# Splitting h for a three-pass matmul: every second high part cast by ScalarE instead of VectorE

## The chip, the cores and the metric

The kernel runs on one core of one Trainium2 chip. The metric is device time in microseconds (us) of one execution, lower is better. The program holds some 28,000 instructions on five engines: TensorE (PE; PEld are its weight loads), VectorE (DVE), ScalarE (ACT), GpSimd (POOL) and SyncE (SP), which here issues the DMAs.

## What is computed

One inference step of a hybrid backbone with one layer, for 128 context tokens and 2,048 latent tokens of width 1,024 with shared weights. In the reference's words, shortened to what matters here:

```
mod = silu(cond) @ ada_w + ada_b ; shift, scale, gate = split(mod, 3)
h = rmsnorm(x, norm_g) * (1 + scale) + shift
p = h @ w_in                      # 2,832 columns: q,k,v, gates, beta, a, u, v, x_c, x_d ...
y_a = gated DeltaNet over chunks of 64 tokens, both directions
y_b = spatial gating MLP ; y_c = pooling ; y_d = real 2-D DFT
y = x + gate * (concat(y_a, y_b, y_c, y_d) @ w_out) ; final rmsnorm
```

## The kernel before

**Three-pass products.** TensorE multiplies in a reduced float format here (fp32r). For the accuracy of float32 every operand is held as a high part, which is a cast of the value, and a low part, which is the value less its high part. `mm3` (L246) issues three matmuls for each product: high by high, high by low, low by high. All of them have line L250.

**Stages.** The tokens are cut into 17 tiles of 128 (the 17th is the context) and these into three groups of 6, 6 and 5 tiles. `phase_a(gi)` (L892) runs for groups 0, 1 and 2, one after the other: it makes h of the group, multiplies it by the weights (`proj_tm`, `proj_cm`), and prepares the DeltaNet chunks, with convolutions (L824), exponentials (L669, L676, L684), 64x64 products (`pair_pre`), and a triangular solve that is spread over lanes on DVE (`lanes_solve` L725 and L727, transposes L748, copies on ACT L757). In the trace phase A takes about the first 500 us. Behind it come the other branches, mixed with the scan over the chunks (`scan`, L1015, matmuls L1035), and the output projection (`out_tile`, also L250).

**How h is made.** `x_prep` (L322) loads x and normalizes it. `x_fin` (L341) goes over the 8 feature blocks f of 128 columns: TensorE transposes up to 512 tokens (L349), ACT applies scale and shift and writes `h` (L351, a buffer out of 4), `h_split` (L358) writes the high part to `hT[0]` (L361, DVE) and the low part to `hT[1]` (L362; POOL for odd f, DVE for even f), and for groups 0 and 1 a DMA keeps h (L355). The tiles `hT` are a part of `BIG`, and there is one copy of them: the next group's f can be written only when the matmuls of the group before have read it. `x_fin` is called seven times: twice for group 0 (384 and 392 tokens), twice for group 1 (384 and 392), three times for group 2 (384, 128, 128). That makes 56 casts and 56 differences. Below, "the first, second, third block" of a group are these calls.

**Who sets the order.** The kernel is written stage by stage, and a scheduler gives every engine its own fixed order before the program runs, by priorities (`tc.high_priority`) and by its own idea of durations. An engine then executes its order strictly one after the other: what waits holds up all that stands behind it on that engine. A changed duration or a changed engine at one place can therefore move instructions elsewhere in the order.

Of the kernel before, what the change touches and what calls it, by code (L numbers as in the profile page):

```python
# [13 lines left out]
AF = mybir.ActivationFunctionType  # L14
# [130 lines left out]
def tile_dit_step(ctx: ExitStack, tc: tile.TileContext, io: dict, dbg=None, stop=None):  # L145
    nc = tc.nc
# [194 lines left out]
    def x_fin(prep, fs=range(KC), pss=(pc,)):  # L341
        with hp(OXv[0]):
            tiles, off, spill, xts = prep
            w = sum(rows for _, rows in tiles)
            cond = 1 if tiles[0][0] == NTS else 0
            for f in fs:
                ps = pss[f % len(pss)]()
                for j, (i, rows) in enumerate(tiles):
                    nc.tensor.transpose(ps[:, j * 128:j * 128 + rows], xts[j][:rows, f * 128:(f + 1) * 128], ident[:rows, :rows])  # L349
                h = hp_.tile([128, 512], F32, tag="pr", name="h", bufs=4)  # L350
                nc.scalar.activation(h[:, :w], ps[:, :w], AF.Identity, scale=modab[:, 0, f, cond:cond + 1],  # L351
                                     bias=modab[:, 1, f, cond:cond + 1])
                h_split(h[:, :w], f, off)
                if spill is not None:
                    nc.sync.dma_start(out=h_d[spill, :, f, off:off + 384], in_=h[:, :384])  # L355
            return h

    def h_split(h, f, off):  # L358
        w = h.shape[1]
        hi = hT[0][:, f, off:off + w]  # L360
        nc.vector.tensor_copy(hi, h)  # L361
        (nc.gpsimd if f % 2 else nc.vector).tensor_tensor(hT[1][:, f, off:off + w], h, hi.bitcast(F32), op=ALU.subtract)  # L362

    def out_dbg(name, ap):
# [1066 lines left out]
```

## Time and profile before

| what | value |
|---|---|
| median of 3 runs | 1192.86 us (1191.8 to 1195.96) |
| the profiled execution | 1198.78 us, its span 1197.0 us |
| PE busy | 1046.3 us (87% of the span) |
| PEld busy | 954.6 us (80%) |
| DVE busy | 818.9 us (68%) |
| ACT busy | 386.2 us (32%) |
| POOL busy | 433.2 us (36%) |
| chain that ended last, by engine | PE 41%, DVE 27%, DMA 17%, issue 6%, ACT 4% |

A profile is one execution. Its instructions have a start and a duration in us from the span's start. An idle time of an engine is shown with what released it: `[2.62 <-DVE tm L708]` means that the engine sat idle for 2.62 us until the DVE instruction of line 708 that wrote `tm` was done.

### The profile page before, as it was taken

What the parts mean: (1) busy time and instruction counts of PE and PEld (TensorE: products, weight loads), DVE (VectorE), ACT (ScalarE), POOL (GpSimd) and SP (SyncE); (2) the same over time, 40 slices, a digit from 0 to 9 for tenths busy, and PEclk for the clock granted to TensorE, in tenths of its full rate; (3) what the DMA queues carried; (4) which work ended last, traced back from release to release, by engine and by line L of the source; (5) the groups of instructions that cost most, each with busy time, mean ns of one, the idle gap of its engine ahead of it and who ended that gap; (6) DMA issues with size and microseconds to landing.
All of it is one profiled execution on the core that took longest, in us unless ns stands there. A gap on an engine that the chain in (4) does not pass through costs nothing.

```text
span 1197.0 us, 27975 instructions
## 1 busy us (share of the span) xinstructions
PE 1046.3 (87%) x11351; PEld 954.6 (80%) x11351; DVE 818.9 (68%) x1837; ACT 386.2 (32%) x734; POOL 433.2 (36%) x436
## 2 busy tenths in 40 slices
PE   4689897888768789967988999888999889999997
PEld 1489786888757788955778888878899879999997
DVE  1547878699995799958865533672443398887765
ACT  1345566436675564131131111121111311111211
POOL 1338446633562245511132132232144444332212
PEclk7599897898978899988899999999999889999998
DMA  9799557854453655565268356578555655444331
GB/s 309 238 327 290 156 117 202 250 165 112 107 134 103 154 126 126 179 170 160 71 197 241 100 170 207 176 230 283 143 151 161 204 153 186 132 142 140 108 131 71
DMA packets 251395, 204.16 MB, mean 171 GB/s; under 512 B 109150, under 2 KB 218718, under 8 KB 251010
## 3 DMA queue, kind: packets, MB, share of 16 engines
q1 hardware_dynamic: 251266, 202.37, 57.7%
q8 instruction: 89, 1.46, 0.5%
q14 instruction: 40, 0.33, 0.1%
HBM read 138.86 MB, written 63.46 MB: 169 GB/s over the span
## 4 chain that ended last, share of the span: by engine, by line
PE 41%; DVE 27%; DMA 17%; issue 6%; ACT 4%; SPq 2%; POOL 2%; DVEq 0%; ACTq 0%; POOLq 0%
PE pj L250 32%; DMA wst<-in_wt_dram 4%; PE pa L1035 3%; DMA ada<-in_ada_dram 3%; DVE LL L727 3%; DVE acc L824 3%; DVE ltmp L725 3%; DMA pr<-in_cpr_dram 2%; DVE BIG L243 2%; DVE BIG L361 1%; DVE acc L871 1%; SPq L1024 1%; DVE BIG L240 1%; DVE BIG L362 1%; DVE LL L748 1%
## 5 line engine op out<-in xcount | busy, mean ns | idle before, releaser
L250 PE MATMUL pj<-BIG 128*128 128x256 f32 (+4 forms) x3888 | 630.8, 319 | 25.6 <-ACT raw L805 5.6
L250 PEld LDWEIGHTS pj<-BIG 128*128 128x128 f32 x3888 | 578.1, 201 | 50.7 <-issue 11.0
L250 PE MATMUL pj<-BIG,yh 128*128 128x256 f32 x1088 | 196.7, 286 | 1.6 <-ACT BIG L1340 0.8
L243 POOL TENSOR_TENSOR BIG<-wst,BIG 128x512 fp32r<-128x512 f32 (+1 forms) x66 | 93.3, 1414 | 215.2 <-DVE BIG L240 131.2
L250 PEld LDWEIGHTS pj<-BIG,yh 128*128 128x128 f32 x1088 | 164.7, 191 | 4.6 <-ACT BIG L1340 1.0
L250 PE MATMUL pj<-BIG,yl 128*128 128x256 f32 x544 | 140.8, 284 | 0.0
L250 PEld LDWEIGHTS pj<-BIG,yl 128*128 128x128 f32 x544 | 99.0, 191 | 0.4
L240 DVE CAST BIG<-wst 128x512 fp32r<-128x512 f32 (+2 forms) x72 | 35.0, 487 | 75.7 <-DMA wst<-in_wt_dram 35.4
L1398 POOL TENSOR_TENSOR z<-z,xs 128x1024 f32<-128x1024 f32 x16 | 40.3, 2521 | 75.8 <-DVE z L1390 66.0
L1042 POOL TENSOR_TENSOR gS<-S,sc_s 128x256 f32<-128x256 f32 x32 | 19.7, 616 | 132.1 <-DVE S L1057 109.1
L824 DVE SCALAR_TENSOR_TENSOR acc<-raw,prm,acc 128x768 f32<-128x768 f32 (+2 forms) x72 | 66.3, 942 | 1.6 <-ACT acc L822 1.6
L243 DVE TENSOR_TENSOR BIG<-wst,BIG 128x512 fp32r<-128x512 f32 (+1 forms) x66 | 49.8, 754 | 24.3 <-ACT BIG L242 20.7
L1359 ACT ACTIVATE yh<-yt 128x768 fp32r<-128x768 f32 (+1 forms) x34 | 20.5, 628 | 121.6 <-issue 65.5
L1204 ACT ACTIVATE g<-pj 128x256 f32<-128x256 f32 (+1 forms) x64 | 23.0, 397 | 109.6 <-PE pj L250 109.3
L725 DVE TENSOR_TENSOR ltmp<-LL 128x60 f32<-128x60 f32 (+14 forms) x90 | 55.5, 617 | 1.6
L727 DVE TENSOR_TENSOR LL<-LL,ltmp 128x60 f32<-128x60 f32 (+14 forms) x90 | 55.3, 615 | 1.5
L242 ACT ACTIVATE BIG<-wst 128x512 fp32r<-128x512 f32 (+1 forms) x60 | 37.7, 633 | 38.4 <-DMA wst<-in_wt_dram 17.9
L264 PE MATMUL pb<-ada,c 128*32 128x256 f32 x192 | 22.1, 566 | 31.7 <-DMA ada<-in_ada_dram 21.4
L1057 DVE TENSOR_TENSOR S<-pa,gS 128x256 f32<-128x256 f32 x34 | 14.3, 421 | 50.6 <-PE pc L1035 45.3
L1390 DVE TENSOR_TENSOR z<-pj,gbc 128x256 f32<-128x256 f32 x68 | 26.2, 420 | 29.1 <-PE pj L250 28.8
L362 POOL TENSOR_TENSOR BIG<-h,BIG 128x384 fp32r<-128x384 f32 (+2 forms) x28 | 29.1, 1041 | 44.5 <-DVE BIG L361 38.7
L1360 DVE TENSOR_TENSOR yl<-yt,yh 128x768 fp32r<-128x768 f32 (+1 forms) x34 | 40.4, 1206 | 4.1 <-ACT yh L1359 3.9
(280 smaller groups left out, 1690.2 us busy)
## 6 DMA issues: line engine op xcount, KB each, us to landing
wst<-in_wt_dram SPq DMA_DIRECT2D x96, 256.0 KB, 3.7
R<-rec_d SPq DMA_DIRECT2D x136, 128.0 KB, 3.0
ada<-in_ada_dram SPq DMA_DIRECT2D x24, 512.0 KB, 8.7
C<-com_d SPq DMA_DIRECT2D x68, 128.0 KB, 3.2
xs<-xs_d SPq DMA_DIRECT2D x16, 512.0 KB, 5.3
out_dram<-z SPq DMA_DIRECT2D x16, 512.0 KB, 3.0
x<-in_xs_dram SPq DMA_DIRECT2D x13, 512.0 KB, 6.4
xs_d<-x SPq DMA_DIRECT2D x13, 512.0 KB, 4.7
```

Of the source, the lines that this page charges most:

```text
L240: nc.vector.tensor_copy(hi[:, ks, a:a + w], st[:, :, :w])
L242: nc.scalar.activation(hi[:, ks, a:a + w], st[:, :, :w], AF.Copy)
L243: (nc.vector if k0 == 0 else nc.gpsimd).tensor_tensor(lo[:, ks, a:a + w], st[:, :, :w], hi[:, ks, a:a + w].bitcast(F32), op=ALU.subtract)
L250: nc.tensor.matmul(out, lh[a](k), rh[b](k), start=(k == first and i == 0), stop=(k == last and i == 2))
L362: (nc.gpsimd if f % 2 else nc.vector).tensor_tensor(hT[1][:, f, off:off + w], h, hi.bitcast(F32), op=ALU.subtract)
L725: nc.vector.tensor_tensor(tv, X[:, :, j, j + 1:32].unsqueeze(2).to_broadcast([128, 2, j, ni]), bc(X[:, :, 0:j, j], ni), op=ALU.mult)
L727: nc.vector.tensor_tensor(X[:, :, 0:j, j + 1:32], X[:, :, 0:j, j + 1:32], tv, op=ALU.add)
L824: nc.vector.scalar_tensor_tensor(o, raw[:, si + j:si + j + n], w[:, j:j + 1], o, op0=ALU.mult, op1=ALU.add)
L1035: nc.tensor.matmul(ps[o, q], lh(q)[hp], rh[hp, q])
L1360: nc.vector.tensor_tensor(yl[:, q], yt[:, q], yh[:, q].bitcast(F32), op=ALU.subtract)
L1390: nc.vector.tensor_tensor(z[:, ns], ps, gbc[:, cd, ns], op=ALU.mult)
L1398: nc.gpsimd.tensor_tensor(z, z, xs, op=ALU.add)
```

## The change

For even f the high part is written by an ACT instruction (a copy with conversion, from SBUF to SBUF), for odd f by DVE as before. The differences stay where they were: DVE for even f, POOL for odd f.

```
     def h_split(h, f, off):
         w = h.shape[1]
         hi = hT[0][:, f, off:off + w]
-        nc.vector.tensor_copy(hi, h)
+        if f % 2:
+            nc.vector.tensor_copy(hi, h)
+        else:
+            nc.scalar.activation(hi, h, AF.Copy)
         (nc.gpsimd if f % 2 else nc.vector).tensor_tensor(hT[1][:, f, off:off + w], h, hi.bitcast(F32), op=ALU.subtract)
```

So 28 of the 56 casts go from DVE to ACT: 12 of 128x384, 8 of 128x392 and 8 of 128x128. Lines behind L361 move down by 3: L364 is the cast on ACT, L362 that on DVE, L365 the difference. The scheduler also gives another order to instructions that the diff doesn't touch, at many places of the program. Three of them follow.

ACT in group 1, the end of the second block. L351 writes h, L684 (L687 after) is an exponential, L711 (L714) copies values that PE has transposed, L911 (L914) takes a product out of PSUM, L242 casts weights. The two L351 rows ahead of the last L711 are those of f = 6 and 7. Before:

```order
L684 ACTIVATE Pf<-Pf 128x1536
L351 ACTIVATE h<-pc,modab 128x392
L242 ACTIVATE BIG<-wst 128x4x128 x2
L351 ACTIVATE h<-pa,modab 128x392
L711 ACTIVATE tm<-pb 128x2x256
L351 ACTIVATE h<-pc,modab 128x392
L351 ACTIVATE h<-pa,modab 128x392
L711 ACTIVATE tm<-pb 128x2x128
L911 ACTIVATE xdt<-pj 128x256 x3
```

and now:

```order
L687 ACTIVATE Pf<-Pf 128x1536
L351 ACTIVATE h<-pc,modab 128x392
L364 ACTIVATE BIG<-h 128x392
L242 ACTIVATE BIG<-wst 128x4x128
L351 ACTIVATE h<-pa,modab 128x392
L914 ACTIVATE xdt<-pj 128x256
L714 ACTIVATE tm<-pb 128x2x256
L914 ACTIVATE xdt<-pj 128x256 x2
L714 ACTIVATE tm<-pb 128x2x128
```

The h of f = 6 and 7, and the cast of f = 6, stand ahead of both L714 copies now. The h of f = 4 and 5 stand further up, ahead of the exponential.

DVE in group 2, the first block, around the transposes that end the triangular solve of group 1 (L748, L751 after; `XT` and `LL` are its tiles). L605 to L623 (L608 to L626) are small steps on the keys' norms, L824 (L827) a convolution. Before, the difference of f = 4 stood ahead of the transposes:

```order
L362 TENSOR_TENSOR BIG<-h,BIG 128x384
L609 TENSOR_TENSOR kt<-eB_1762,kt 128x12
L610 TENSOR_TENSOR kt<-be_1759,kt 128x24
L623 SCALAR_TENSOR_TENSOR S_1768<-eB_1762,kt 128x12
L748 STREAM_TRANSPOSE XT<-LL 128x32x32 x2
```

and now, where the two L365 rows are the differences of f = 2 and f = 4:

```order
L751 STREAM_TRANSPOSE XT<-LL 128x32x32 x2
L362 CAST BIG<-h 128x384
L827 SCALAR_TENSOR_TENSOR acc<-raw,prm,acc 128x768
L243 TENSOR_TENSOR BIG<-wst,BIG 128x4x136
L751 STREAM_TRANSPOSE LL<-LL 128x32x32
L365 TENSOR_TENSOR BIG<-h,BIG 128x384
L751 STREAM_TRANSPOSE LL<-LL 128x32x32
L362 CAST BIG<-h 128x384
L608 SCALAR_TENSOR_TENSOR kt<-kt,P_1758 128x24
L620 SCALAR_TENSOR_TENSOR Pp_1763<-kt,P_1758 128x24
L827 SCALAR_TENSOR_TENSOR acc<-raw,prm,acc 128x768
L365 TENSOR_TENSOR BIG<-h,BIG 128x384
```

The transposes have moved ahead of two of the differences that PE needs.

ACT at the same place. L757 (L760 after) copies the transposed solution, four pieces at a time. Before:

```order
L602 ACTIVATE kt<-kt,eps 128x12
L603 ACT_TABLE_LOAD
L603 ACTIVATE kt<-kt 128x12
L242 ACTIVATE BIG<-wst 128x4x136
L242 ACTIVATE BIG<-wst 128x4x128
L351 ACTIVATE h<-pc,modab 128x384
L351 ACTIVATE h<-pa,modab 128x384
L757 ACTIVATE XF<-XT 32x2x12x32 x4
```

and now:

```order
L605 ACTIVATE kt<-kt,eps 128x12
L760 ACTIVATE XF<-XT 32x2x12x32 x4
L364 ACTIVATE BIG<-h 128x384
L606 ACT_TABLE_LOAD
L606 ACTIVATE kt<-kt 128x12
L351 ACTIVATE h<-pc,modab 128x384
L242 ACTIVATE BIG<-wst 128x4x136
L351 ACTIVATE h<-pa,modab 128x384
L760 ACTIVATE XF<-LL 32x2x12x32 x4
L364 ACTIVATE BIG<-h 128x384
```

The casts of f = 4 and f = 6 each stand directly behind a set of four copies, which in turn wait for DVE's transposes.

## Rows read from the trace of the kernel before

**Rows 1.** Busy time by stretch: start:end, length, then PE, PEld, DVE, ACT, POOL, PEclk, DMA share, GB/s

```profile
46.00:68.00 22.00, 19.68 (x136) 17.98 (x129) 19.44 (x36) 12.56 (x22) 11.59 (x9) 0.81 0.65 220
68.00:90.00 22.00, 18.48 (x121) 16.79 (x120) 7.91 (x21) 9.93 (x20) 8.99 (x11) 0.92 1.02 351
...
160.00:213.00 53.00, 42.77 (x354) 37.90 (x353) 45.10 (x83) 34.65 (x59) 29.60 (x30) 0.85 0.66 169
213.00:295.00 82.00, 72.75 (x585) 69.15 (x585) 70.02 (x132) 37.00 (x65) 34.72 (x33) 0.94 0.61 172
295.00:375.00 80.00, 60.66 (x406) 54.63 (x405) 71.00 (x140) 49.54 (x83) 41.01 (x46) 0.82 0.50 118
```

**Rows 2.** The same stretches, DVE's casts of line L361 alone

```profile
46.00:68.00 22.00, 4.34 (x8) 0.81 0.65 220
68.00:90.00 22.00, 3.00 (x8) 0.92 1.02 351
...
160.00:213.00 53.00, 10.20 (x16) 0.85 0.66 169
...
295.00:375.00 80.00, 9.46 (x24) 0.82 0.50 118
```

**Rows 3.** Timeline of DVE and POOL: start, duration, engine, line, operation, tiles, shapes

```profile
49.31 1.44 DVE L361 CAST BIG<-h 128x384 fp32r<-128x384 f32 x1
...
365.62 0.22 DVE L361 CAST BIG<-h 128x128 fp32r<-128x128 f32 x1
...
48.93 1.61 POOL L298 TENSOR_TENSOR x<-x,cpc 128x512 f32<-128x512 f32 x1 [0.94 <-DMA x<-in_xs_dram]
```

**Rows 4.** Timeline of ACT: instructions of two widths

```profile
160.07 0.53 ACT L676 ACTIVATE Po<-Po 128x384 f32<-128x384 f32 x1
...
225.75 0.24 ACT L534 ACTIVATE bl<-lg 128x48 f32<-128x48 f32 x1 [0.43 <-DVE lg L912]
```

**Rows 5.** Timeline of ACT, group 1, end of the second block

```profile
202.46 1.49 ACT L684 ACTIVATE Pf<-Pf 128x1536 f32<-128x1536 f32 x1 [3.32 <-DVE Pf L683]
...
208.73 0.60 ACT L711 ACTIVATE tm<-pb 128x512 f32<-128x512 f32 x1 [2.62 <-DVE tm L708]
209.23 0.67 ACT L351 ACTIVATE h<-pc,modab 128x392 f32<-128x392 f32 x1
```

**Rows 6.** Timeline of DVE and PE at the same place

```profile
207.42 0.68 DVE L243 TENSOR_TENSOR BIG<-wst,BIG 128x512 fp32r<-128x512 f32 x1
208.02 0.68 DVE L708 TENSOR_TENSOR tm<-pb,be 128x512 f32<-128x512 f32 x1
...
209.36 0.41 DVE L708 TENSOR_TENSOR tm<-pb,be 128x256 f32<-128x256 f32 x1
209.93 0.42 DVE L361 CAST BIG<-h 128x392 fp32r<-128x392 f32 x1 [0.16 <-ACT h L351]
210.38 1.26 DVE L362 TENSOR_TENSOR BIG<-h,BIG 128x392 fp32r<-128x392 f32 x1
...
212.47 0.32 DVE L912 COPY lg<-pj 128x16 f32<-128x16 f32 x3
...
212.69 11.69 PE L250 MATMUL pj<-BIG 128*128 128x272 f32 x72 [3.30 <-DVE lg L912]
```

**Rows 7.** Timeline of DVE, PE and ACT, group 2, first block

```profile
324.14 0.61 DVE L361 CAST BIG<-h 128x384 fp32r<-128x384 f32 x2
...
335.18 3.81 DVE L748 STREAM_TRANSPOSE XT<-LL 128x1024 f32<-128x1024 f32 x2
...
348.86 1.82 DVE L362 TENSOR_TENSOR BIG<-h,BIG 128x384 fp32r<-128x384 f32 x1
...
350.73 3.09 PE L250 MATMUL pj<-BIG 128*128 128x272 f32 x12 [4.50 <-DVE BIG L362]
...
337.26 3.40 ACT L757 ACTIVATE XF<-XT 32x768 f32<-32x768 f32 x4 [3.19 <-DVE XT L748]
```

**Rows 8.** The chain of waits: start, duration, piece

```profile
1066.33 11.50 PE pj L250 x96
```

## The prediction

> **What bounds the kernel now.** I read the busy time by stretch first, with the same view of line L361 alone beside it, then the timelines of ACT, DVE and PE at the four places where h is made, and the chain of waits last. The program touches h between 46 and 375 us alone, in four stretches. In 46 to 68 DVE is busy 19.44 of 22 us; in 68 to 90 the DMA engines are full (share 1.02) while DVE does 7.91; in 160 to 213, group 1, DVE is busy 45.10 of 53 us and PE 42.77; in 295 to 375, group 2, DVE 71.00 of 80 and PE 60.66 [rows 1]. In the last two PE waits for h while DVE works almost without a gap, and the granted clock is 0.85 and 0.82 there, against 0.94 in the stretch between them. That stretch, 213 to 295, has PE busy for 72.75 of 82 us: there PE comes first, so a start that is earlier by some us is handed on. ACT has 18 us of idle time in the one DVE-bound stretch and 30 in the other [rows 1].
>
> **What is removed.** Casts of L361 occupy DVE for 4.34, 3.00, 10.20 and 9.46 us in the four stretches, 27.0 together [rows 2]. Half of them by count go, so about 13.5 us by their mean. But a cast that nothing disturbs takes 0.30 us for 128x384 (0.61 for two) and 0.22 for 128x128 [rows 3, 7]; 20 x 0.30 + 8 x 0.22 = 7.8 us. The other 5.7 us are casts that wait inside their own duration: the one at 49.31 takes 1.44 us and ends at 50.75, right behind POOL's addition, which runs from 48.93 to 50.54 [rows 3]. Whether these come back depends on what DVE has next.
> The Trainium skill ("SBUF — State Buffer", section "SBUF: two separate sides") says that DVE and GpSimd share one pair of ports as an exclusive lock, for a DVE instruction that uses both ports or has two SBUF inputs. The rows agree with it in the 1.44 us. By that rule the difference that follows, with its two SBUF inputs, would meet the same POOL instruction, the wait would only change its owner, and group 2 below would give 3.0 us where I take 3.5.
>
> **What is added.** 28 instructions on ACT. Nearest rows: 0.53 us for 128x384 from SBUF to SBUF and 0.24 for 48 columns [rows 4]; the line through the two gives 0.31 for 128. So 20 x 0.53 + 8 x 0.31 = 13.1 us on ACT: 4.2 in group 0, 4.2 in group 1, 2.1 + 2.5 in group 2. A copy needs no new table: in the order's rows the casts L242 and L364 stand behind an exponential without an ACT_TABLE_LOAD.
>
> **Group 0 (46 to 90 us): 0.** Up to 58 us DVE is the late one, and it loses half of 4.34 us. But what comes next is a stretch in which the DMA engines are full, with the loads of the next x among what they move [rows 1]. These loads are issued in the order of SP's queue, whose stores of h and x change places here with about the same bytes ahead of them. I take 0, with bounds of (4.34 + 3.00) / 2 = 3.7 us gained, all that DVE loses, and 4.2 us lost, all that ACT gets.
>
> **Group 1 (160 to 213): 3.3 us gained.** PE's 72 matmuls at 212.69 wait for the small copies L912, which stand on DVE behind the casts and differences of the second block [rows 6]. These are late because ACT's h of f = 6, at 209.23, stands behind a copy L711 that waits 2.62 us for DVE [rows 5]. In the new order f = 6 and its cast follow the exponential, which ends at 202.46 + 1.49 = 203.95. Then h 0.67 and the cast 0.53 end at 205.15; on DVE the difference (up to 1.26), L708 (0.68), L243 (0.68), L708 (0.41) and the cast of f = 7 (0.42) end at 208.6, and the L912 with 0.32 at 208.9 [rows 5, 6]. With four hand-overs of 0.1 us, about the 0.16 of DVE's idle time at 209.93 [rows 6], that is 209.3; before it was 212.47 + 0.32 = 212.8. The difference, 3.5 us, I cut to 3.3, since PE may itself be late with the product that L914 takes out of PSUM. The seven other casts put 3.7 us on ACT ahead of this, and take 10.20 / 2 = 5.1 us from DVE. ACT was waiting for DVE as often as the reverse, so I count these two at nothing; the bounds are their full sizes, 3.7 lost and 5.1 gained.
>
> **Group 2 (295 to 375): 3.5 us gained.** PE's last long wait in the first block, 4.50 us, ends with the difference of f = 6, which ends at 350.68 [rows 7]. From the cast of f = 1 at 324.14 to there DVE runs through. In the new order the same work lies between these two, without the casts of f = 2, 4 and 6 and with one weight difference moved behind: 3 x 0.30 + 0.68 = 1.6 us less [rows 6, 7]. The casts of the two small blocks give 8 x 0.22 = 1.8 us, of which the second block's 0.9 lie on DVE's path. By the mean of rows 2 the twelve casts would give 9.46 / 2 = 4.7; by the short ones 4 x 0.30 + 1.8 = 3.0. I take 3.5, nearer to the short ones. What is late next: the difference of f = 2, which before stood ahead of all transposes, now stands behind three of them, 3 x 3.81 / 2 = 5.7 us. With the weight difference (0.68) and some four wide instructions of about 1 us (0.68 for 512 columns) it comes, by this estimate, 11 us behind the cast of f = 1, and 12 to 14 us ahead of f = 6 [rows 6, 7]. In these PE has the matmuls of f = 2 to 5: 3 tiles x 4 features x 3 = 36 at 3.09 / 12 = 0.26 us make 9.3 us [rows 7], so it fits. Bounds: 4.7 gained, and on the other side the second rival.
>
> **Sum.** 3.3 + 3.5 = 6.8 us. Behind 375 us nothing is removed or added; the order differs, and PE's work is the same. On the profiled execution, 1198.78 us, that gives 1192.0. It lies 5.9 us above the median of the runs shown; on that, 1192.86 - 6.8 = **1186.0 us**, 0.6% less. A measurement here tells about 0.3%, 3.6 us, from no change.
>
> **Rivals.**
> 1. *All of DVE's time comes back.* Both DVE-bound stretches hand on the mean price, 5.1 + 4.7, and group 0 its 3.7: 13.5 us, 1179.4. For it: DVE has no gap in group 2. Against it: waits on POOL change owner, and DMA is full in group 0.
> 2. *ACT's queue becomes the late one.* In group 2 the casts of f = 4 and 6 stand behind sets of copies of 3.40 us each, which wait for DVE's transposes (3.19 us at 337.26) [rows 7]. Price: 2 x 3.40, and in group 1 the 3.7 us on ACT: 10.5 lost, less the 3.3 of the moved h: +7.2, 1200.1 us. It decides from the point at which DVE reaches a difference before ACT has its cast. Against it: by the same count of rows some 12 us of DVE's work lie between the third transpose and the difference of f = 6, and some 9 between the first two and that of f = 4, where ACT needs 3.40 + 0.53 for copies and cast. For it: every early h and every new table ahead of these copies uses up that slack.
> 3. *The tail takes it.* In PE's new order 72 more projection matmuls stand ahead of the first scan step; at 11.50 / 96 = 0.12 us [rows 8] it starts 8.6 us later beside the projections. If the scan's own chain set the end, the result would be 1186.0 + 8.6 = 1194.6, no change. Against it: counted in the new order, 984 matmuls of line L250 still stand behind the scan's last step, 118 us of work, so that PE sets the end.
> 4. *Hidden.* DMA and the solve on DVE take the place of every wait removed: 1192.9.
>
> **Chances.** My forecast, a gain between 3.6 and 10 us: 0.40. Rival 1, or something near it: 0.15. Rivals 3 and 4, within 3.6 us: 0.24. Slower by more: 0.21, rival 2 with 0.13 and other shifts of the order, each priced from no row, with 0.08. So faster 0.55, same 0.24, slower 0.21. The range goes from 1175, a little under rival 1 for the 4.2 us or so by which group 0 may add, to 1200, rival 2; I leave out about 2 in 10 on both sides together.
>
> **What would show it.** Right: DVE's busy time falls by 9 to 14 us and ACT's rises by about 13; PE's 72 matmuls of group 1 start 3 us earlier and those behind f = 6 of group 2 about 7 us earlier than before, and this lead is still there at 500 us. The wait of 2.62 us for L708 no longer stands ahead of an h. Wrong: an ACT cast with a long wait in front of it whose difference is what DVE or PE waits for (rival 2); a lead at 375 us that is gone at 640 or 930 (rival 3); or no lead at 213 (rival 4).

## The result: 0.74% slower, and the profile after

| | median | runs | ratio to before, 95% interval |
|---|---|---|---|
| before | 1195.09 us | 20 | |
| after | 1203.79 us (1198.51 to 1210.42) | 20 | 1.0074 (1.0056 to 1.0091) |

The change costs about 8.7 us. I had forecast 1186.0 us with a range of 1175 to 1200: the sign is wrong, and the result lies outside the range. (My base was the median of the first 3 runs; 20 runs put it 2.2 us higher.) The profiled execution after took 1202.52 us, its span 1200.7 us, only 3.7 us more than the one before; single executions of one kernel spread over some 10 us, so sizes below come from many runs or from means over several profiles, and a single profile is used for places.

The page after, busy time of each engine:

```profile
PE 1044.3 (87%) x11351; PEld 955.5 (80%) x11351; DVE 822.7 (69%) x1809; ACT 396.7 (33%) x762; POOL 443.7 (37%) x436
```

ACT has 28 instructions more and is busy 10.5 us longer. DVE has 28 instructions fewer and is busy 3.8 us longer all the same; POOL, with the same instructions, 10.5 us longer. The view by stretch of after, which answers to [rows 1] (columns as there):

```profile
46.00:68.00 22.00, 19.97 (x132) 19.58 (x132) 17.90 (x35) 14.03 (x29) 11.08 (x9) 1.00 0.63 211
160.00:213.00 53.00, 42.96 (x388) 38.15 (x387) 40.66 (x75) 38.12 (x66) 25.58 (x26) 0.87 0.67 166
213.00:295.00 82.00, 74.77 (x578) 72.24 (x579) 73.75 (x135) 38.86 (x70) 38.62 (x37) 0.94 0.65 176
295.00:375.00 80.00, 58.51 (x371) 51.97 (x372) 66.21 (x124) 50.74 (x90) 45.73 (x45) 0.79 0.50 115
```

Where h is made, DVE did get lighter (45.10 to 40.66 us in group 1, 71.00 to 66.21 in group 2). PE got nothing of it: in 295 to 375 it does 58.51 us where it did 60.66. The stretch between, 213 to 295, has DVE at 73.75 after 70.02, which fits work of group 1 that is done later.

The casts on ACT (line L364 of after alone: stretch, length, ACT's busy time):

```profile
46.00:68.00 22.00, 2.06 (x4) 1.00 0.63 211
68.00:90.00 22.00, 2.13 (x4) 0.92 0.96 318
160.00:213.00 53.00, 4.20 (x8) 0.87 0.67 166
295.00:375.00 80.00, 4.25 (x11) 0.79 0.50 115
```

That is 12.6 us for 27 of them (the last lies behind 375 us), against 13.1 forecast for 28.

**Group 1**, timelines of ACT, DVE and PE after, which answer to [rows 5, 6]:

```profile
207.32 1.49 ACT L687 ACTIVATE Pf<-Pf 128x1536 f32<-128x1536 f32 x1 [1.48 <-DVE Pf L686]
208.72 0.66 ACT L351 ACTIVATE h<-pc,modab 128x392 f32<-128x392 f32 x1
209.41 0.53 ACT L364 ACTIVATE BIG<-h 128x392 fp32r<-128x392 f32 x1
...
209.97 1.04 DVE L365 TENSOR_TENSOR BIG<-h,BIG 128x392 fp32r<-128x392 f32 x1 [1.45 <-ACT BIG L364]
...
212.75 0.32 DVE L915 COPY lg<-pj 128x16 f32<-128x16 f32 x3
...
212.96 9.31 PE L250 MATMUL pj<-BIG 128*128 128x272 f32 x72 [1.33 <-DVE lg L915]
```

h of f = 6 does stand right behind the exponential now, but the exponential begins at 207.32 and not at 202.46. So the 72 matmuls start at 212.96 (before: 212.69).

**Group 2**, timelines of ACT, DVE, POOL and PE after, which answer to [rows 7]:

```profile
339.32 0.52 ACT L364 ACTIVATE BIG<-h 128x384 fp32r<-128x384 f32 x1
...
325.90 3.67 DVE L751 STREAM_TRANSPOSE XT<-LL 128x1024 f32<-128x1024 f32 x2
...
330.62 0.71 DVE L243 TENSOR_TENSOR BIG<-wst,BIG 128x544 fp32r<-128x544 f32 x1
...
345.56 0.55 DVE L365 TENSOR_TENSOR BIG<-h,BIG 128x384 fp32r<-128x384 f32 x1
...
360.44 0.92 DVE L319 SCALAR_TENSOR_TENSOR rr<-rt,rr 128x1 f32<-128x1 f32 x1
...
363.91 0.75 DVE L338 TENSOR_SCALAR x<-x,rr 128x1024 f32<-128x1024 f32 x1
...
342.97 5.79 POOL L365 TENSOR_TENSOR BIG<-h,BIG 128x384 fp32r<-128x384 f32 x1
...
331.38 6.65 PE L250 MATMUL pj<-BIG 128*128 128x272 f32 x31 [3.74 <-DVE BIG L243]
...
348.82 1.16 PE L250 MATMUL pj<-BIG 128*128 128x272 f32 x7 [1.76 <-POOL BIG L365]
...
364.71 0.47 PE L349 MATMUL pc<-cm,x 128*128 128x128 f32 x1 [3.88 <-DVE x L338]
```

DVE's difference of f = 6 ends at 346.1, 4.6 us earlier than in [rows 7]. But PE's matmuls wait 3.74 us for a weight difference that now stands behind two transposes, then 1.76 us for POOL's difference of an odd f, which takes 5.79 us, then 3.88 us for the scaled x (L338). What was won on DVE is gone there; the same instruction of the kernel before:

```profile
363.37 0.75 DVE L338 TENSOR_SCALAR x<-x,rr 128x1024 f32<-128x1024 f32 x1
```

**The end.** The chain of waits after, which answers to [rows 8]:

```profile
1072.38 8.69 PE pj L250 x72
...
1082.15 11.53 PE pj L250 x96
```

From there PE runs almost without a gap, as before. So the loss lies ahead of it.

### The profile page after: what moved, and what is told of

Its sections match the earlier page's. It is cut to its first block, busy times and chain, and to the rows that moved or that the text cites. A ratio compares the mean times of both kernels' runs of the same rounds, so it can differ in the third digit from the quotient of the medians.

```text
span 1200.7 us, 27973 instructions
## 1 busy us (share of the span) xinstructions
PE 1044.3 (87%) x11351; PEld 955.5 (80%) x11351; DVE 822.7 (69%) x1809; ACT 396.7 (33%) x762; POOL 443.7 (37%) x436
## 4 chain that ended last, share of the span: by engine, by line
PE 40%; DVE 28%; DMA 17%; issue 6%; POOL 4%; ACT 3%; SPq 2%; DVEq 0%; ACTq 0%; POOLq 0%
PE pj L250 31%; PE pa L1038 3%; DVE ltmp L728 3%; DVE acc L827 3%; DMA pr<-in_cpr_dram 3%; DVE LL L730 3%; DMA wst<-in_wt_dram 3%; DMA ada<-in_ada_dram 2%; DVE BIG L243 2%; DMA yt<-y_d 1%; POOL BIG L243 1%; DVE BIG L240 1%; DVE acc L874 1%; DVE yl L1363 1%; DMA raw_d<-yd 1%
## 5 line engine op out<-in xcount | busy, mean ns | idle before, releaser
L250 PE MATMUL pj<-BIG 128*128 128x256 f32 (+4 forms) x3888 | 627.7, 318 | 27.7 <-DVE BIG L243 6.3
L250 PEld LDWEIGHTS pj<-BIG 128*128 128x128 f32 x3888 | 575.9, 200 | 49.3 <-issue 8.2
L250 PE MATMUL pj<-BIG,yh 128*128 128x256 f32 x1088 | 195.9, 286 | 2.4 <-ACT BIG L1343 1.4
L243 POOL TENSOR_TENSOR BIG<-wst,BIG 128x512 fp32r<-128x512 f32 (+1 forms) x66 | 100.1, 1516 | 216.7 <-DVE BIG L240 121.4
L250 PEld LDWEIGHTS pj<-BIG,yh 128*128 128x128 f32 x1088 | 163.2, 190 | 5.9 <-ACT BIG L1343 1.6
L250 PE MATMUL pj<-BIG,yl 128*128 128x256 f32 x544 | 138.5, 283 | 0.0
L250 PEld LDWEIGHTS pj<-BIG,yl 128*128 128x128 f32 x544 | 97.4, 190 | 0.3
L240 DVE CAST BIG<-wst 128x512 fp32r<-128x512 f32 (+2 forms) x72 | 41.0, 571 | 70.6 <-DMA wst<-in_wt_dram 32.6
L827 DVE SCALAR_TENSOR_TENSOR acc<-raw,prm,acc 128x768 f32<-128x768 f32 (+1 forms) x72 | 64.1, 913 | 0.1
L365 POOL TENSOR_TENSOR BIG<-h,BIG 128x384 fp32r<-128x384 f32 (+2 forms) x28 | 36.8, 1314 | 59.9 <-DVE BIG L362 54.1
L1363 DVE TENSOR_TENSOR yl<-yt,yh 128x768 fp32r<-128x768 f32 (+1 forms) x34 | 49.5, 1475 | 13.5 <-ACT yh L1362 13.5
L242 ACT ACTIVATE BIG<-wst 128x512 fp32r<-128x512 f32 (+1 forms) x60 | 37.8, 634 | 32.3 <-DMA wst<-in_wt_dram 20.4
```

Of the source, the lines that this page charges most:

```text
L240: nc.vector.tensor_copy(hi[:, ks, a:a + w], st[:, :, :w])
L242: nc.scalar.activation(hi[:, ks, a:a + w], st[:, :, :w], AF.Copy)
L243: (nc.vector if k0 == 0 else nc.gpsimd).tensor_tensor(lo[:, ks, a:a + w], st[:, :, :w], hi[:, ks, a:a + w].bitcast(F32), op=ALU.subtract)
L250: nc.tensor.matmul(out, lh[a](k), rh[b](k), start=(k == first and i == 0), stop=(k == last and i == 2))
L827: nc.vector.scalar_tensor_tensor(o, raw[:, si + j:si + j + n], w[:, j:j + 1], o, op0=ALU.mult, op1=ALU.add)
L1363: nc.vector.tensor_tensor(yl[:, q], yt[:, q], yh[:, q].bitcast(F32), op=ALU.subtract)
```

## The experiments

The one line changes two things: where the casts run, and the order of all five engines. To take them apart, a table with the number of each instruction was added to the kernel, and between neighbours on an engine an edge that fixes the order and adds no wait:

```
     with _tile.TileContext(nc, schedule_with_timeline_sim=True) as tc:
         tile_dit_step(tc, io)
+        _pin(tc)
...
+    for n in np.cumsum(todo).tolist():
...
+            tc.add_manual_dep(i, p, mybir.DependencyInfo(mybir.DependencyClass.NoSync, mybir.DependencyReason.DATA), reason="pin")
+        prev[i.engine] = i.name
```

The kernels differ in `h_split` and in this table. "Old" is the order of the kernel before, "new" that of after; a cut is made at one instruction of the whole list. Ratios are to the kernel before on the same chip; its medians there were 1192.7 to 1196.3 us. No run has the table with an unchanged order. That it costs nothing by itself is read from casts_only, which has it and isn't slower, and from weights_first below, which has the new order but for one instruction and lies at 1.0083, where the change without the table lies at 1.0074 and 1.0098.

| kernel | casts on ACT | 0 to 89 us | 89 to 213 | 213 to 375 | 375 to scan | scan to end | median us | ratio (95%) |
|---|---|---|---|---|---|---|---|---|
| casts_only | even f | old | old | old | old | old | 1193.23 | 0.9988 (0.9965 to 1.0010) |
| order_only | none | new | new | new | new | new | 1213.24 | 1.0149 (1.0124 to 1.0174) |
| after_again | even f | new | new | new | new | new | 1204.18 | 1.0098 (1.0063 to 1.0132) |
| head_new | even f | new | new | new | old | old | 1196.69 | 1.0023 (1.0001 to 1.0046) |
| tail_new | even f | old | old | old | new | new | 1195.00 | 1.0000 (0.9976 to 1.0023) |
| new_to_scan | even f | new | new | new | new | old | 1197.07 | 1.0046 (1.0018 to 1.0075) |
| scan_new | even f | old | old | old | old | new | 1199.09 | 1.0052 (1.0031 to 1.0072) |
| group01_new | even f | new | new | old | old | old | 1198.81 | 1.0057 (1.0033 to 1.0082) |
| group0_new | even f | new | old | old | old | old | 1193.21 | 1.0009 (0.9991 to 1.0026) |
| group1_new | even f | old | new | old | old | old | 1197.18 | 1.0044 (1.0020 to 1.0068) |
| group1_late | even f | old | new from 146 | old | old | old | 1198.80 | 1.0024 (1.0000 to 1.0049) |
| group2_new | even f | old | old | new | old | old | 1196.31 | 1.0025 (1.0003 to 1.0048) |
| casts_all | all | old | old | old | old | old | 1192.46 | 0.9979 (0.9956 to 1.0001) |

### Casts and order apart: casts_only, order_only, head_new, tail_new, after_again

> The 28 casts of even f go to ScalarE, and every engine keeps the order of the kernel before for all other instructions (a table with the number of each instruction adds one order-only edge per neighbour on an engine); a cast stands on ScalarE at the place in the whole list that it had on VectorE. Theory 1 (the reshuffled order costs the time, above all behind the last h at 375 us): none of the 8.7 us is there; within 0.3% of the kernel before, or up to 7 us faster. Theory 2 (the casts themselves cost it, in ScalarE's queue): about 8.7 us slower, ratio 1.007. Theory 3 (the order of the first 375 us costs it): as theory 1.

> All 56 casts stay on VectorE, and every engine is held to the order of the changed kernel; a cast stands on VectorE at the place in the whole list that it had on ScalarE. Theory 1 (the reshuffled order costs the time, above all behind 375 us): slower by 8 to 13 us, ratio 1.007 to 1.011. Theory 2 (the casts themselves): within 0.3% of the kernel before. Theory 3 (the order of the first 375 us): as theory 1.

> The change in the first 375 us alone: casts on ScalarE and the changed kernel's order for what the kernel before issues up to its last difference of h; behind that the order of the kernel before. Theory 1 (the loss lies in the order behind 375 us): within 0.3% of the kernel before or faster by up to 7 us. Theories 2 and 3 (casts, or the order of the first 375 us): slower by about 8.7 us, ratio 1.007.

> Casts on ScalarE, the order of the kernel before up to the last difference of h, and behind that the order of the changed kernel. Theory 1 (the loss lies in the order behind 375 us): slower by about 8.7 us, ratio 1.007. Theory 2 (the casts themselves): slower by 8.7 us here and in the two other kernels with casts on ScalarE. Theory 3 (the order of the first 375 us): within 0.3% of the kernel before.

> The changed kernel once more, with the edit written on one line, on the chip of the next three. If the parts add up (a new order of the first 375 us costs about 4 us against the casts alone, the new order behind it about 1.5), it lies 4 us over the kernel before, ratio 1.003 to 1.005; if new head and new tail cost more together than apart, 7 to 10 us over it, ratio 1.006 to 1.009.

Without the reshuffle the casts cost nothing: 0.9988. The order without the casts costs 1.5%, more than the change itself, so theory 2 (the casts, ACT's queue) falls. (order_only's 1.0149 lies above the 1.007 to 1.011 that theory 1 gave.) Where the order costs it, these five don't say: neither half alone reaches the loss, head_new fits neither forecast, and after_again shows that the loss is real, with 1.0098 above both of its forecasts. The page of casts_only:

```profile
PE 1042.8 (87%) x11351; PEld 946.8 (79%) x11351; DVE 805.1 (68%) x1809; ACT 396.8 (33%) x762; POOL 440.4 (37%) x436
```

DVE is 13.8 us less busy than before, just what the mean price of the casts had promised. In the new order the very same 1809 instructions take 822.7 us (821.8 in after_again): 17.6 us more, all of it in longer durations.

### The scan stage: new_to_scan, scan_new, small_eight, scan_early

small_eight has no table; it lets the scheduler order a smaller edit, shown here. scan_early has all casts on ACT and a table whose order behind about 600 us prefers the scan.

```
-        nc.vector.tensor_copy(hi, h)
+        (nc.scalar.activation(hi, h, AF.Copy) if f % 2 == 0 and w == 128 else nc.vector.tensor_copy(hi, h))
```

> Casts on ScalarE; the changed kernel's order for all that the kernel before issues up to its first scan step, the order of the kernel before from there on (the 72 projection matmuls that the change draws ahead of the first scan step are behind it again). Theory 4 (the rest of the loss comes from the scan stage: 72 matmuls fewer lie between the scan steps, and PE waits inside the steps): as the new head alone, ratio 1.000 to 1.004. Theory 5 (it comes from where the new head meets the new order of 375 to 640 us): 7 to 9 us slower, ratio 1.006 to 1.009.

> Casts on ScalarE; the order of the kernel before up to the first scan step (with the 72 projection matmuls that the change draws ahead of it), the changed kernel's order from there on. Theory 4 (the scan stage): slower than the casts alone by 4 to 6 us, ratio 1.002 to 1.005, and PE's idle time from 740 to 880 us is 5 us longer than with the casts alone. Theory 5: no slower than the casts alone, ratio 0.996 to 1.001.

> Only the eight 128x128 casts of even f in group 2 go to ScalarE, and the scheduler orders the program by itself. It again puts 72 projection matmuls ahead of the first scan step, as the change does, while the order of the first 300 us stays nearly that of the kernel before. Theory 4 (the 72 matmuls and the thinner scan stage cost time): slower by 2 to 6 us, ratio 1.002 to 1.005. Rival (only the head's order costs time): ratio 0.998 to 1.001.

> All 56 casts on ScalarE; the order is the kernel before's up to about 600 us, and behind that one in which the scan is preferred, so that 24 projection matmuls fewer stand ahead of its first step. Theory 4 (72 more cost 5 us, so 24 fewer give about 1.5 us): ratio 0.994 to 0.998. Rival (the kernel before already has the scan early enough): as casts_all, 0.997 to 1.000.

small_eight: 1200.41 us, ratio 1.0043 (1.0020 to 1.0066). scan_early: 1194.46 us, 1.0016 (0.9993 to 1.0039), above both of its forecasts.

With eight casts of 0.2 us moved at 345 to 375 us, the program is 0.43% slower; the scheduler again draws 72 projection matmuls ahead of the first scan step. Taken back, as in new_to_scan, the loss halves (1.0046, between the forecasts of theories 4 and 5). Put in alone, as in scan_new, it appears. tail_new is the one that doesn't fit, at 1.0000. The three kernels with the old head and the new scan stage average 1.0032, those with the new head and the old scan stage (head_new, new_to_scan, three_back below) 1.0032 too. From 0.9988 that is 0.44% for either half, and 0.9988 + 0.0044 + 0.0044 = 1.0076, where after shows 1.0074 and after_again 1.0098. With intervals of 0.2% and more to either side, that the halves add up is a reading which the runs allow, not one that they prove.

In time: over the seven profiles of kernels with the 72 matmuls ahead, the scan starts 263.3 us after the last L912 of phase A, over the eleven with the casts moved and the old place 256.6. From the scan's start to the end PE then has 72 matmuls less to do, 8.6 us by [rows 8], but that stretch takes 548.0 us after 549.6. So 6.7 us are paid and 1.6 come back. Where the rest stays shows when the stretch is cut at the scan's last step. The view by stretch of after, then of casts_only (columns as in [rows 1]):

```profile
642.40:1068.90 426.50, 395.80 (x5229) 362.84 (x5228) 243.22 (x634) 74.91 (x167) 140.49 (x123) 0.96 0.58 177
1068.90:1200.70 131.80, 123.54 (x1144) 121.48 (x1134) 90.16 (x262) 24.47 (x47) 32.71 (x24) 0.99 0.32 113
```

```profile
636.20:1051.70 415.50, 388.87 (x5212) 356.81 (x5214) 235.36 (x632) 75.80 (x174) 135.79 (x123) 0.97 0.60 182
1051.70:1192.70 141.00, 132.66 (x1235) 130.62 (x1226) 96.19 (x278) 26.34 (x50) 35.73 (x25) 0.98 0.33 115
```

The 72 matmuls come from behind the scan's last step, and there PE is busy 9.1 us less, near the price (123.6 us after 132.7, in the means). Between the steps stand as many projection matmuls as ever (2,180 after 2,178), yet the scan takes 424.4 us after 416.9, and the two sets of profiles don't overlap: 421.3 to 426.5 against 414.8 to 418.8. Little of these 7.5 us is PE standing idle, 29.9 us after 28.3. PE is busy longer, 394.5 us after 388.6, and so is DVE, 241.6 after 235.5; the granted clock (1 is its full level) is 0.977 after 0.991 in the first 100 us of the scan and 0.951 after 0.966 in the 140 behind them, in the means. (The one profile of the kernel before has 421.5 us from first to last step, so a single execution doesn't show it.) Why nearly the same work between the scan's steps takes longer is open.

scan_new was to show PE's idle time from 740 to 880 us 5 us longer than casts_only; it is 3.2 us longer. In the other direction scan_early found nothing: 24 matmuls fewer ahead of the scan are no gain, 0.4% over casts_all.

### The head: which group's order costs

> Casts on ScalarE; the changed kernel's order for all that the kernel before issues up to the L912 copy that ends group 1's projection (212.8 us), the order of the kernel before from there on. If the head's 4 us come from group 2's order (295 to 375 us): as the casts alone, ratio 0.996 to 1.001. If they come from groups 0 and 1: ratio 1.001 to 1.004. My prediction had group 1's order gain 3.3 us: then ratio 0.994 to 0.998.

> Casts on ScalarE; the changed kernel's order up to the sixth L912 copy (89 us, group 0's h), the order of the kernel before from there on. If the head's 5 us come from the order in which group 0's h, its loads and stores stand: ratio 1.002 to 1.006. If they come from behind it (the kt chain and what follows in 90 to 213 us): as the casts alone, 0.996 to 1.001.

> Casts on ScalarE; the changed kernel's order only between the sixth and the ninth L912 copy (89 to 213 us, with group 1's h), the order of the kernel before ahead of it and behind it. If the late kt chain of 141 to 188 us carries the head's loss: ratio 1.002 to 1.006. If group 0 does: 0.996 to 1.001. By my prediction's step for group 1 alone: a gain of 3.3 us, 0.995 to 0.997.

> Casts on ScalarE; the changed kernel's order only between the first L613 (146 us) and the ninth L912 copy (213 us), where group 1's h is made; the order of the kernel before ahead of it and behind it. If the order around group 1's h carries the loss of group1_new: ratio 1.002 to 1.006. If the stretch from 89 to 146 us does (loads, kt chain of the first pair): 0.997 to 1.001.

> Casts on ScalarE; the changed kernel's order only between the ninth L912 copy (213 us) and the last difference of h (375 us), the order of the kernel before ahead of it and behind it. By my prediction's step for group 2 alone: a gain of 3.5 us, ratio 0.995 to 0.998. If GpSimd's long difference at 343 us and the scaling of x behind it take the gain, as in the changed kernel's trace: 0.998 to 1.003.

Group 0's order costs nothing that can be measured. Group 1's does: group1_new and group01_new lie 0.56% and 0.69% over casts_only, so the step for which I had forecast a gain of 3.3 us is one that loses. In the profile of group1_new the 72 matmuls of [rows 6] are no later than with the casts alone (the last of those L912 ends at 211.7 us in both); the time goes in the stretch behind, from there to the last L912 of phase A, 168.0 us after 165.2. The other profiles agree: about 168 to 172 us in all ten with the new order of group 1, 163 to 167 in those with the old order of both groups (group2_new, with group 2's alone, 168). What fits is DVE's work that is put off: L613 of the first pair stands at 153.5 us in after, behind wide instructions, and at 144.9 in casts_only. But group1_late, which has only half of the stretch, lies in the middle, and three_back, below, moved that very instruction without a gain that can be told. So the stretch is shown, the instruction is not. Group 2's order costs rather than gains, by an interval that just excludes no change to the kernel before.

Two kernels put single places of the new order back. weights_first moves one DVE instruction; three_back also moves the chain around L613 and takes the old order from the scan on.

```
 L601 TENSOR_REDUCE kt<-tm 128x12
+L243 TENSOR_TENSOR BIG<-wst,BIG 128x4x136
 L748 STREAM_TRANSPOSE XT<-LL 128x32x32 x2
 L361 CAST BIG<-h 128x384
 L824 SCALAR_TENSOR_TENSOR acc<-raw,prm,acc 128x768
-L243 TENSOR_TENSOR BIG<-wst,BIG 128x4x136
```

> The changed kernel's order with one instruction moved: on VectorE the weight difference L243 (128x544) that stands behind two 1024-wide transposes L748 in group 2 is put ahead of them, where the kernel before has it. Theory 6 (this place costs group 2 its time: PE's 31 matmuls at 331.4 us wait 3.7 us for it, and the kt chain and GpSimd's work behind them come late with it): those matmuls start 3 to 4 us earlier, the scaling of x L338 at 363.9 is 3 to 6 us earlier too, and the kernel is 3 to 5 us faster than the changed one, ratio to the kernel before 1.003 to 1.007. Rival: GpSimd's difference of 5.8 us at 343 holds PE anyway; the lead is gone by 380 us, ratio 1.007 to 1.010.

> The changed kernel's order with three places put back: the move of weights_first; on VectorE the small kt chain and L613 of group 0's first pair ahead of L682 again; and from the first scan step on the order of the kernel before. Theory 7 (the loss sits in a few places that can be named): as fast as the casts alone, ratio 0.996 to 1.002. Theory 8 (it is spread over many small displacements): 1.003 or more.

weights_first: 1205.72 us, 1.0083 (1.0058 to 1.0108), no better than the changed kernel: the rival is right. three_back: 1199.39 us, 1.0026 (1.0001 to 1.0051), no clear gain on new_to_scan (1.0046) and between the forecasts of theories 7 and 8, nearer to 8. The timelines of PE and POOL of weights_first at the moved instruction show why:

```profile
328.33 4.23 PE L250 MATMUL pj<-BIG 128*128 128x272 f32 x21
334.93 2.64 PE L250 MATMUL pj<-BIG 128*128 128x272 f32 x10 [2.36 <-DVE BIG L362]
...
344.85 4.49 PE L250 MATMUL pj<-BIG 128*128 128x272 f32 x21 [5.54 <-POOL BIG L243]
...
337.25 6.26 POOL L362 TENSOR_TENSOR BIG<-h,BIG 128x384 fp32r<-128x384 f32 x1 [3.88 <-DVE BIG L361]
343.47 1.32 POOL L243 TENSOR_TENSOR BIG<-wst,BIG 128x544 fp32r<-128x544 f32 x1
```

PE's matmuls start 3 us earlier than in after (328.33, not 331.38) and then wait 5.54 us for POOL's weight difference, which stands behind a difference of 6.26 us. The wait changed its place and its owner.

### All casts on ACT: casts_all, casts_all_again

```
-        nc.vector.tensor_copy(hi, h)
+        nc.scalar.activation(hi, h, AF.Copy)
```

> All 56 casts on ScalarE, every other instruction in the order of the kernel before. If VectorE's time is worth something where PE waits for h: VectorE's busy time falls by 10 to 14 us more, and the time by 1 to 4 us against the casts of even f alone, ratio 0.994 to 0.998. If ScalarE's queue becomes the late one: 2 to 6 us more, ratio 1.000 to 1.005. If h is hidden behind other waits: no difference to the casts alone.

> casts_all once more: all 56 casts on ScalarE, the order of the kernel before. If it is faster than the kernel before: ratio 0.996 to 0.999. If the first measurement was chance: 0.999 to 1.002.

casts_all_again: 1191.59 us, 0.9971 (0.9940 to 1.0002). With casts_all's 0.9979 that is a gain of 0.25%, 3 us, and both intervals just touch no change. Against casts_only (0.9988) no gain can be told. casts_all is the fastest kernel of the study, about 1% faster than the change. The page of casts_all has DVE 11.1 us under casts_only:

```profile
PE 1043.2 (88%) x11351; PEld 951.1 (80%) x11351; DVE 794.0 (67%) x1781; ACT 406.6 (34%) x790; POOL 437.7 (37%) x436
```

So taking 25 us of DVE's busy time where PE waits for h is worth some 3 us, if it is worth anything. That other waits stand close behind is the reading that fits; no run tests it.

## Why the prediction was wrong

**What was removed and added: right in the order of before, wrong in the new one.** I had 13.5 us off DVE by the mean of [rows 2] and 13.1 us onto ACT. casts_only shows 13.8 off, so the 5.7 us of waits inside the casts were saved there too, though POOL's busy time rose by 7.2 us. The change itself put 12.6 us on ACT for 27 casts, but DVE's busy time rose by 3.8 us where I had named a fall of 9 to 14 as the sign of being right: the reshuffle gave back more than the casts had taken. The Trainium skill ("SBUF — State Buffer", section "SBUF: two separate sides") says that the port pair that DVE and GpSimd share is held for a whole instruction. By it I had the waits only change their owner; POOL's 7.2 us are in line with that and DVE's 13.8 are not. Both that reading and my step took the order as fixed.

**Group 0, nothing: right.** The first L912 copies came 3.6 us earlier in after, and 0.4 us at 88 us, behind the stretch that DMA fills (share 0.96). group0_new and casts_only can't be told apart.

**Group 1, 3.3 us gained: failed**, at the step that takes "the exponential, which ends at 202.46 + 1.49" from the old trace. The exponential begins 4.86 us later, at 213 us nothing is gained (212.96 after 212.69), and behind it group 1's order costs 0.56%. The exponential waits for DVE's products, and these for the kt chain (the small steps on the keys' norms), which was moved by the same reshuffle. The reduction at its head, before and then after:

```profile
178.53 0.94 DVE L601 TENSOR_REDUCE kt<-tm 128x12 f32<-128x768 f32 x1
```

```profile
182.35 0.95 DVE L604 TENSOR_REDUCE kt<-tm 128x12 f32<-128x768 f32 x1 [4.64 <-ACT tm L601]
```

In the new order ACT writes its input later, and DVE stands idle for it, 2.6 to 4.6 us in all ten profiles with the new order of group 1 and in none of the others. From there to the exponential DVE has hardly a gap. No run puts this place back alone. From the exponential's end to that of L912 (here L915) my working holds: 4.3 us (208.81 to 213.07) where it gave 5.4 (203.95 to 209.3). I moved one wait and held what it waits for fixed.

**Group 2, 3.5 us gained: failed at "what is late next".** The size on DVE was right or too small (f = 6's difference 4.6 us earlier). I looked for the next late one among DVE's differences of even f; it was POOL's of an odd f (5.79 us at 342.97; 1.01 us for the last of that width in casts_only), DVE's weight difference of 128x544 behind the transposes, which I had counted only as work ahead of f = 2 and not as something that PE waits for, and the scaling of x.

**"Behind 375 us nothing is removed or added; the order differs, and PE's work is the same": failed.** This zero was wrong by about 5 us, by the ratios. Rival 3 had its first half, 72 matmuls and 8.6 us (measured 6.7), but not the mechanism: it needed the scan's own chain to set the end. PE sets the end, as I had argued, with 984 matmuls of line L250 behind the scan's last step, and that part is shorter by the price of the 72. The time is lost between 375 us and there, in a later start of the scan and in a scan that takes 7.5 us longer.

**Rival 2**, ACT's queue, didn't come. In after the cast of f = 6 does stand behind its copies, but it ends at 339.84, 5.7 us before DVE reaches its difference at 345.56. order_only loses without a cast on ACT, and casts_all, in the old order, loses nothing with twice as many. What came, other shifts of the order, had 0.08 of my chances, without a price.

**Open.** Which instructions of group 1's order cost the 0.6%, why the scan takes longer, why tail_new lost nothing, and why order_only is 0.5% to 0.75% slower than the change; its casts stand on DVE at places made for ACT.

## What to carry to other kernels

When a scheduler sets the order, a one-line change is two changes: time them apart, by pinning the old order with the new instruction in it, before the instruction is praised or blamed. Here the edit alone was free and the reshuffle cost 0.9%; with even eight casts of 0.2 us moved, 72 matmuls changed place and the program was 0.4% slower. In a prediction, a term for the order belongs in the sum, and a wait that is moved must be costed with its producer moved too.

## What the runs showed of the hardware that I had not expected

How long a POOL or DVE instruction takes depended on its neighbour far more than I had allowed. The last POOL difference of 128x384 in group 2 and its neighbour on DVE, and the small steps on DVE that scale x, in casts_only and then in after (POOL's difference of after is shown above, at 342.97):

```profile
339.69 1.01 POOL L362 TENSOR_TENSOR BIG<-h,BIG 128x384 fp32r<-128x384 f32 x1 [2.70 <-DVE BIG L361]
339.54 2.08 DVE L748 STREAM_TRANSPOSE LL<-LL 128x1024 f32<-128x1024 f32 x1
...
358.33 0.16 DVE L318 SCALAR_TENSOR_TENSOR rt<-rt,rv 128x1 f32<-128x1 f32 x1
358.53 0.16 DVE L319 SCALAR_TENSOR_TENSOR rr<-rt,rr 128x1 f32<-128x1 f32 x1
```

```profile
342.95 0.94 DVE L685 TENSOR_TENSOR Pf<-Pf,Pn 128x768 f32<-128x768 f32 x1
...
347.63 0.28 DVE L365 TENSOR_TENSOR BIG<-h,BIG 128x128 fp32r<-128x128 f32 x1
...
361.39 0.75 DVE L317 TENSOR_TENSOR rt<-rr 128x1 f32<-128x1 f32 x1
362.18 0.92 DVE L318 SCALAR_TENSOR_TENSOR rt<-rt,rv 128x1 f32<-128x1 f32 x1
...
361.30 0.83 POOL L678 TENSOR_TENSOR Po<-Q,Po 128x384 f32<-128x384 f32 x1
362.09 0.99 POOL L671 TENSOR_TENSOR Pd<-Pd,cm 128x384 f32<-128x384 f32 x1
```

Beside one of DVE's transposes POOL's difference takes 1.01 us. In after it takes 5.79 us, beside a run of DVE instructions without a gap, most of them sums, products and differences of two tensors, from 342.95 to 347.91; it ends 0.85 us behind that run. The 6.26 us of weights_first look the same: DVE's run ends at 342.65 and POOL's difference at 343.51. A DVE step on 128x1 takes 0.16 us alone and 0.75 to 0.92 beside POOL's, and each ends with POOL's. So which instructions fall beside each other is itself a cost of the order. Between two orders of the same program DVE's busy time differs by 17.6 us; how much of it comes from such neighbours isn't counted.
